# A decoder block on one core: sums' pieces at other steps, each chunk's combination tied to its own place, w_out's raw rows in four buffers

## The chip, the core and the metric

The kernel runs on one core of one Trainium2 chip. The metric is the device time of one execution in microseconds (us), from start to end; less is better. A core has five engines, each with its own instruction queue that is worked strictly in order: TensorE (PE, matrix products), VectorE (DVE), ScalarE (ACT), GpSimd (POOL) and SyncE (SP, which here only issues transfers). Transfers (DMAs) can be issued from the queues of SP, ACT and POOL. Engines wait for each other only through semaphores; a waiting instruction holds up everything behind it in its queue.

## What is computed

The reference is a decoder block with model width 1024 and 2048 tokens, all in float32:

```python
h = _rmsnorm(x, norm_pre_mix)
proj = h @ w_in                                  # q, k, v, u, z, gate_a, gate_b
y_attn = dilated attention of q, k, v            # 3 patterns x 4 heads, merged by softmax of the log-denominators
y_gmlp = gelu(u) * (causal 128x128 mix of layernorm(gelu(z)))
merged = sigmoid(gate_a) * (y_attn @ w_branch_attn) + sigmoid(gate_b) * (y_gmlp @ w_branch_gmlp)
x = x + _rmsnorm(merged @ w_out, norm_post_mix)
h = _rmsnorm(x, norm_pre_mlp)
x = x + _rmsnorm(relu(h @ w_mlp_in) ** 2 @ w_mlp_out, norm_post_mlp)
```

The three attention patterns each leave their own output, maximum and denominator per token. They are combined at the end: `y_attn = sum over patterns of softmax(log-denominator) * output`.

## The kernel before, in words

**Products.** A float32 operand is cut into a high and a low half (`split`, L67: a rounded copy on ACT or POOL, then a subtraction on DVE or POOL at L78), and a product is three matmuls (high x high, high x low, low x high; L95 to L97). The gates' and the MLP's products save one in eight with sums of operand blocks, which have to be made first.

**Order.** PE's instructions run in the order in which the Python code issues them (L56). The other engines' queues are ordered by a planner, which takes what is ready first in its own model of time; `with behind():` (L174) narrows this: every instruction in the block is queued after the last one that the code had issued on the same engine.

**Stages around the change.**

1. Projections. `v_block` (L338) computes v for 128 tokens, `qk_pair` (L301) one third of q or k for 512 tokens. Tokens come in four chunks c = 0 to 3 of 512, and the two halves (chunks 0 and 1, then 2 and 3) are done one after the other.
2. Beside them the **sums** for the gates are made in pieces. `pre_s` (L447) takes a part of w_in (one load of 512 KB on SP, four DVE additions at L455 to L458, two stores on POOL's queue), `pre_t` (L431) the same for the normalized input (two loads of 256 KB, four DVE additions at L439 to L442, one store). Each is a generator of three parts: load, add, store. `pre_step` (L469), inside `behind()`, starts the next piece's load, does the additions of the piece before and the store of the one before that. The list `makers` (L465) has 28 pieces, and eight more (for the first half's input) are put behind it at L519. `while flow: pre_step()` (L517) does all that is left of the 28 when the projections are through.
3. The **filler** (`filler`, L739): u (64 steps), z of the second half (two chunks of 32 steps, `z_chunk`, L565), the gates (505 steps) and z of the first half (64 steps). A step is three matmuls of 128x512. `spatial` (L522) loads the gMLP's mixing weights `wsp`, masks them on POOL (L533) and, after 72 steps of filler, lets PE make a row sum of them (L538). `sz_out` (L547) mixes a normalized chunk of z; it is issued late in the next chunk.
4. **Attention** (`attn_unit`, L830): 48 units, between whose parts steps of the filler are put, so that PE has something to do while the softmax runs. What is left of the gates then, 75 steps, stands beside the **combination** (`combine`, L933), one generator for each chunk: first part, three loads of 528 KB (L937); second part, the weights and the weighted sum (about twenty DVE instructions and an exp on ACT, L940 to L957, then two additions of 128x1024 at L959 and L960, on DVE for chunks 1 and 2, on POOL for 0 and 3); third part, eight PE transposes (L965), a copy on ACT (L967) and a store.
5. **The gates' own work.** `gates` (L661) goes through 126 blocks t of four steps. Block t loads the raw weights of block t + 4 (`piece`, L608), splits those of block t + 3 (`split_piece`, L625), and after its matmuls adds its result on DVE (L723 to L729) or copies it on ACT; results are stored at the end of the next block (L711). From `LAST` = 116 on, each block takes a PSUM bank of its own, of four.
6. **Merge** (`merge`, L1106): for each of eight column tiles dt of a chunk, 18 matmuls, gating on DVE (L1120, L1122). In the first chunk's merge w_out is fetched and split too (`spatial_out`, L1405, which calls `split_wo`, L1063): raw rows of 128x1024 into two buffers "y1", the next load when a buffer is free. From L1139 on `out_block` multiplies by w_out.

Of the kernel before, what the change touches and what calls it, by code (L numbers as in the profile page):

```python
# [16 lines left out]
P = 128  # L17
S = 2048
D = 1024
# [22 lines left out]
def block_kernel(ctx, tc, a, out):  # L42
# [319 lines left out]
    with ExitStack() as e1a:  # L362
# [102 lines left out]
        makers = [lambda n=n, k=k: pre_s(n, k) for n in range(10) for k in (0, 2)]  # L465
        makers[12:12] = [lambda z=z: pre_t(*z) for z in halves[1]]
        flow = []
# [13 lines left out]
        for half in range(2):  # L481
# [4 lines left out]
            for n, (c, i) in enumerate(mine):  # L486
                nb = mine[n + 1] if n + 1 < len(mine) else None
                between = None
                if nb and not (half and nb[0] == 2):
                    if nb != (0, 1):  # L490
                        prenorm_rows(*nb)
                    between = lambda nb=nb: prenorm_cols(*nb)
                v_block(rp, wv, c, i, between)
                if (c, i) == (0, 1):
                    first.close()
# [3 lines left out]
            for n, (g, which) in enumerate(qk):  # L499
# [14 lines left out]
                pre_step()  # L514
                if half and n % 3 == 2:
                    pre_step()
        while flow:  # L517
# [107 lines left out]
    def split_piece(t):  # L625

        if t >= len(seq):
            return
        if t == 4:
            g_["spots"].append(wp.tile([P, 4, 2, 4, P], F32R, name="spots1", tag="w", bufs=3))  # L630
        at_ = t % 4 if t >= LAST else t % 8
        w = g_["spots"][at_ // 4][:, at_ % 4]
        split(w[:, 0], w[:, 1], g_["raw"].pop(t).rearrange("p (k c) -> p k c", k=4),
              "act" if t < 12 or t > LAST - 10 else "pool", "pool")
        g_["w"][t] = w
# [25 lines left out]
    def gates():  # L661
# [75 lines left out]
        yield  # L737

    def filler():  # L739

        for q, (wi, kind, n, half) in enumerate(queue):
# [11 lines left out]
            if kind == "z":  # L753
                if not half:
                    reload_h(1)
                for ci in range(2):
                    for k, _ in enumerate(z_chunk(zps[half], w, half * 2 + ci)):
                        yield
                        if half and k == 10 and (makers or flow):
                            pre_step()  # L760
                    if half and not ci:
                        gates_ahead()
                continue
            for c in (2, 3):
                for m in range(2):
                    p = psum_mm(f"u_{n}{m}{c}")
                    yield from steps_T(w, m, c, p)
                    t = st.tile([P, 512], F32, name=f"ut_{n}{m}{c}", tag="ev", bufs=3)
                    act.activation(t, p, AF.Gelu_apprx_tanh)
                    sp.dma_start(u_d[n * 2 + m, :, c * 512:(c + 1) * 512], t)  # L770
                    pre_step()

# [160 lines left out]
    def combine(c):  # L933
# [20 lines left out]
        for i in range(4):  # L954
            for g in range(3):
                o = A[:, i, g, 0:256].rearrange("p (j e) -> p j e", j=4)
                dve.tensor_tensor(o, o, widen(E[:, i, g, :], 64), op=OP.mult)  # L957
        eng = dve if c in (1, 2) else pool
        eng.tensor_add(A[:, :, 0, :256], A[:, :, 0, :256], A[:, :, 1, :256])  # L959
        eng.tensor_add(A[:, :, 0, :256], A[:, :, 0, :256], A[:, :, 2, :256])  # L960
        yield
# [57 lines left out]
    cs = [combine(c) for c in (2, 3, 0, 1)]  # L1019
    for n in range(2):  # L1020
        for z in cs:
            next(z)
    for n in range(4):
        steps((40, 12, 12, 11)[n])
        next(cs[n])
    ec.close()
# [32 lines left out]
    def load_wo(k):  # L1059
        wo_raw[k] = bot.tile([P, D], F32, name=f"woraw{k}", tag="y1", bufs=2)  # L1060
        (sp if k < 2 else pool).dma_start(wo_raw[k], a["w_out"][:, k, :])

    def split_wo(k):  # L1063
        split(wo[k][:, 0], wo[k][:, 1], wo_raw.pop(k))
        if k + 2 < KT:
            load_wo(k + 2)

# [337 lines left out]
    def spatial_out(dt):  # L1405
# [4 lines left out]
        if dt == 1:  # L1410
            ez.close()
            mgp.append(stack(e2, "mg1", 1))
            ttp = stack(e2r, "ttp", 2, side="right")
        split_wo(dt)
        if dt == KT - 1:
# [591 lines left out]
```

## Time and profile before

| what | value |
|---|---|
| three runs | 2676.23, 2681.05 and 2683.57 us, median 2681.05 |
| the profiled execution: its own time | 2676.26 us |
| its span, first to last instruction | 2674.5 us (1.8 us lie around it) |
| PE busy | 2621.4 us, 12458 matmuls |
| DVE, ACT, POOL busy | 1677.4, 1077.5 and 1196.8 us |
| moved by DMA | 521.99 MB, mean 195 GB/s |
| mean granted TensorE clock | 0.993 |

Times in the trace are us from the first instruction. A row of the timeline has the start, the duration, the engine, the line of the kernel, the operation and `out<-in` by the program's names, then the number of instructions that were merged into the row, and in square brackets how long the engine had been idle before it and what ended that. SPq is SP's queue of transfers; its durations are those of issuing. A row of waits has: who waited, for whom, us in total, times, the longest. A row of windows has the stretch and its length, then busy us and (number) for PE, PEld (weight loads), DVE, ACT and POOL, then the granted clock, the DMA share and GB/s.

### The profile page before, as it was taken

To read this page: it belongs to the slowest core of one execution; us is meant where nothing else is said; L and a number is where in the kernel's file an instruction comes from. 1 tells how busy PE (TensorE), PEld (TensorE's weight loads), DVE (VectorE), ACT (ScalarE), POOL (GpSimd) and SP (SyncE) were. 2 spreads that over 40 slices of the span, in tenths; PEclk is the share of its full clock that TensorE was granted. 3 is DMA by queue.
4 is the path that set the end of the run, shared out by engine and by line. 5 is a ranking of instruction groups with operands and counts; after the bars stand their busy time and mean duration, and the time that the engine had idled before them with its cause. 6 is when DMAs were issued, how large, how long until landed. Compare 5 with 4: busy or idle time off the path is not lost. (4 is left out here: it accounts for less than half of the span.)

```text
span 2674.5 us, 35483 instructions
## 1 busy us (share of the span) xinstructions
PE 2621.4 (98%) x12458; PEld 2188.0 (82%) x12458; DVE 1677.4 (63%) x2881; ACT 1077.5 (40%) x2184; POOL 1196.8 (45%) x1078
## 2 busy tenths in 40 slices
PE   9999999899999978999999999999999999999998
PEld 8888888788888867788878788888888888888886
DVE  5675565445544556665676665655437888888866
ACT  5213111244455332354445555555545333233334
POOL 0362354365455544310333464223315776676645
PEclk9999999999999999999999999999999999999999
DMA  8778668888898987743666464654343212222235
GB/s 322 279 248 276 246 227 280 271 277 261 293 287 237 240 260 271 267 165 136 213 224 255 130 224 153 209 155 129 106 147 117 87 57 86 87 87 87 87 111 212
DMA packets 387843, 521.99 MB, mean 195 GB/s; under 512 B 56849, under 2 KB 241937, under 8 KB 385874
## 3 DMA queue, kind: packets, MB, share of 16 engines
q1 hardware_dynamic: 300048, 431.84, 49.2%
q0 software_dynamic: 14992, 51.65, 5.0%
q10 hardware_dynamic: 72626, 36.25, 4.5%
q8 instruction: 98, 1.61, 0.2%
q14 instruction: 79, 0.65, 0.1%
HBM read 340.67 MB, written 178.98 MB: 194 GB/s over the span
## 5 line engine op out<-in xcount | busy, mean ns | idle before, releaser
L1858 PE MATMUL ya<-T_spots,s 128*128 128x512 f32 x1176 | 289.3, 389 | 0.7 <-ACT T_spots L70 0.5
L70 ACT ACTIVATE s<-sraw 128x768 fp32r<-128x768 f32 (+1 forms) x184 | 127.2, 696 | 330.4 <-POOL sraw L1659 156.1
L1858 PEld LDWEIGHTS ya<-T_spots,s 128*128 128x128 f32 x1176 | 220.5, 188 | 47.4 <-ACT T_spots L70 0.9
L78 DVE TENSOR_TENSOR s<-sraw,s 128x512 fp32r<-128x512 f32 x172 | 184.5, 1097 | 8.5 <-ACT s L70 7.2
L698 PE MATMUL g<-opA,spots 128*128 128x512 f32 x672 | 171.8, 400 | 12.7 <-DVE ga L723 12.7
L1333 PE MATMUL aa<-B,A 128*128 128x512 f32 x768 | 182.4, 390 | 0.9 <-DVE A L85 0.7
L1304 POOL TENSOR_TENSOR s<-w1r 128x512 f32<-128x512 f32 x32 | 42.3, 1322 | 309.8 <-DVE S L78 263.1
L698 PE MATMUL g<-opB,spots 128*128 128x512 f32 x648 | 168.3, 403 | 6.1 <-DVE gx L729 4.6
L1333 PEld LDWEIGHTS aa<-B,A 128*128 128x128 f32 x768 | 143.9, 188 | 31.4 <-DVE A L85 1.1
L1858 PE MATMUL yc<-T_spots,s 128*128 128x512 f32 x624 | 159.6, 389 | 0.0
L698 PEld LDWEIGHTS g<-opA,spots 128*128 128x128 f32 x672 | 122.2, 190 | 35.1 <-issue 13.1
L95 PE MATMUL x<-hT_a,wq 128*128 128x512 f32 x384 | 149.7, 390 | 0.0
L96 PE MATMUL x<-hT_a,wq 128*128 128x512 f32 x384 | 149.4, 389 | 0.0
L97 PE MATMUL x<-hT_a,wq 128*128 128x512 f32 x384 | 149.4, 389 | 0.0
L78 POOL TENSOR_TENSOR spots<-gr,spots 128x512 fp32r<-128x512 f32 x98 | 130.3, 1335 | 41.3 <-ACT spots L70 26.7
L698 PEld LDWEIGHTS g<-opB,spots 128*128 128x128 f32 x648 | 118.6, 192 | 29.5 <-issue 5.0
L1858 PEld LDWEIGHTS yc<-T_spots,s 128*128 128x128 f32 x624 | 117.1, 188 | 24.3
L70 ACT ACTIVATE hl<-r 128x512 fp32r<-128x512 f32 x48 | 30.4, 633 | 240.2 <-POOL r L322 89.0
L1658 POOL TENSOR_TENSOR sraw<-sraw 128x256 f32<-128x256 f32 x56 | 41.9, 748 | 161.5 <-DVE s L78 158.5
L72 POOL TENSOR_SCALAR wq<-wq_r 128x1024 fp32r<-128x1024 f32 x24 | 31.5, 1317 | 184.1 <-PE va L97 133.4
L929 DVE TENSOR_REDUCE o<-po 128x256 f32<-128x512 f32 x48 | 33.2, 692 | 121.2 <-PE po L928 121.2
L78 POOL TENSOR_TENSOR T_spots<-w2r,T_spots 128x512 fp32r<-128x512 f32 x70 | 104.5, 1522 | 7.3 <-ACT T_spots L70 7.3
(412 smaller groups left out, 6988.8 us busy)
## 6 DMA issues: line engine op xcount, KB each, us to landing
w1r<-in_w_mlp_in_dram SPq DMA_DIRECT2D x64, 512.0 KB, 3.7
sraw<-sd SPq DMA_DIRECT2D x128, 256.0 KB, 3.3
qk<-hl SPq DMA_DIRECT2D x24, 1024.0 KB, 5.5
qq<-qk SPq DMA_DIRECT2D x96, 256.0 KB, 5.0
w2r<-in_w_mlp_out_dram SPq DMA_DIRECT2D x16, 1024.0 KB, 7.7
sd<-u ACTq DMA_DIRECT2D x63, 256.0 KB, 2.9
g<-gated SPq DMA_DIRECT2D x58, 256.0 KB, 3.7
gr<-sgd SPq DMA_DIRECT2D x53, 256.0 KB, 4.7
```

Of the source, the lines that this page charges most:

```text
L70: act.activation(hi, src, AF.Copy)
L72: pool.tensor_scalar(hi, src, 1.0, 1.0, op0=OP.mult, op1=OP.mult)
L78: (pool if lo_eng == "pool" else dve).tensor_sub(lo, src, f32(hi))
L95: pe.matmul(ps, lh, rh, start=start, stop=False)
L96: pe.matmul(ps, lh, rl, start=False, stop=False)
L97: pe.matmul(ps, ll, rh, start=False, stop=stop)
L698: pe.matmul(p, w[:, l, k], h[:, r, k], start=i in (1, 6, 5, 4) and not k and not m, stop=k == 3 and m == 2, skip_group_check=True)
L929: dve.tensor_reduce(ot[:, :, j * 64:(j + 1) * 64], po.rearrange("p (b h e) -> p b e h", b=4, h=2), axis=AX.X, op=OP.add)
L1304: pool.tensor_add(s1, a21, a22)
L1333: pe.matmul(p, w[:, l, k, :], h[:, r, k, :], start=i in (1, 6, 5) and not k and not n, stop=k == 3 and n == 2, skip_group_check=True)
L1658: pool.tensor_add(a22, a21, a22)
L1858: pe.matmul(p, s[:, l], w[r], start=i in (1, 2, 5) and not m and not o, stop=m == 1 and o == 2, skip_group_check=True)
```

## The change

It has three parts.

- **Sums.** The pieces of the second half's input stand at places 16 to 23 of `makers`, not 12 to 19. `pre_step` is also called after every second `v_block` of the second half (4 calls more) and no longer twice extra in the second half's q and k (2 calls fewer). In the filler a helper `paced` calls it after every 12th step of u and z, where it was called after every 8th step of u and once in each of the two chunks of z; both make ten calls.
- **Combination.** All four chunks' loads are still issued at the end of attention. The second parts, which all four came right behind, now come at 28, 38, 48 and 58 of the 75 steps, the third parts at 42, 52, 63 and 75 (before: 40, 52, 64, 75), each inside `behind()`. The additions are cut in two: four of 128x512 in place of two of 128x1024. Three rounded copies (blocks 107 to 109) go from ACT to POOL.
- **w_out.** Raw rows 2 and 3 (and 6 and 7) get two buffers "tt" of the pool `ttp`, which is opened at dt = 1 in the place of z's buffers; rows 4 and 5 are loaded when rows 0 and 1 are split.

```diff
@@ -463,7 +463,7 @@
 
         halves = [[(h_, k, j) for k in range(4) for j in range(2)] for h_ in range(2)]
         makers = [lambda n=n, k=k: pre_s(n, k) for n in range(10) for k in (0, 2)]
-        makers[12:12] = [lambda z=z: pre_t(*z) for z in halves[1]]
+        makers[16:16] = [lambda z=z: pre_t(*z) for z in halves[1]]
         flow = []
 
         def pre_step():
@@ -491,6 +491,8 @@
                         prenorm_rows(*nb)
                     between = lambda nb=nb: prenorm_cols(*nb)
                 v_block(rp, wv, c, i, between)
+                if half and i % 2:
+                    pre_step()
                 if (c, i) == (0, 1):
                     first.close()
             nxt = load_w(0, f"wq00{half}")
@@ -512,8 +514,6 @@
                     between = lambda i: prenorm_cols(2, i)
                 qk_pair(rp, w, g, which, 2 * half + 1, ropes[2 * half + 1], between)
                 pre_step()
-                if half and n % 3 == 2:
-                    pre_step()
         while flow:
             pre_step()
         makers += [lambda z=z: pre_t(*z) for z in halves[0]]
@@ -631,7 +631,7 @@
         at_ = t % 4 if t >= LAST else t % 8
         w = g_["spots"][at_ // 4][:, at_ % 4]
         split(w[:, 0], w[:, 1], g_["raw"].pop(t).rearrange("p (k c) -> p k c", k=4),
-              "act" if t < 12 or t > LAST - 10 else "pool", "pool")
+              "act" if t < 12 or t > LAST - 7 else "pool", "pool")
         g_["w"][t] = w
 
     def operand(half, i, slot):
@@ -736,6 +736,16 @@
         sp.dma_start(*out_.pop())
         yield
 
+    paces = [0]
+
+    def paced(gen):
+
+        for _ in gen:
+            yield
+            paces[0] += 1
+            if paces[0] % 12 == 0 and (makers or flow):
+                pre_step()
+
     def filler():
 
         for q, (wi, kind, n, half) in enumerate(queue):
@@ -754,21 +764,17 @@
                 if not half:
                     reload_h(1)
                 for ci in range(2):
-                    for k, _ in enumerate(z_chunk(zps[half], w, half * 2 + ci)):
-                        yield
-                        if half and k == 10 and (makers or flow):
-                            pre_step()
+                    yield from paced(z_chunk(zps[half], w, half * 2 + ci))
                     if half and not ci:
                         gates_ahead()
                 continue
             for c in (2, 3):
                 for m in range(2):
                     p = psum_mm(f"u_{n}{m}{c}")
-                    yield from steps_T(w, m, c, p)
+                    yield from paced(steps_T(w, m, c, p))
                     t = st.tile([P, 512], F32, name=f"ut_{n}{m}{c}", tag="ev", bufs=3)
                     act.activation(t, p, AF.Gelu_apprx_tanh)
                     sp.dma_start(u_d[n * 2 + m, :, c * 512:(c + 1) * 512], t)
-                    pre_step()
 
     fill = filler()
 
@@ -955,9 +961,10 @@
             for g in range(3):
                 o = A[:, i, g, 0:256].rearrange("p (j e) -> p j e", j=4)
                 dve.tensor_tensor(o, o, widen(E[:, i, g, :], 64), op=OP.mult)
-        eng = dve if c in (1, 2) else pool
-        eng.tensor_add(A[:, :, 0, :256], A[:, :, 0, :256], A[:, :, 1, :256])
-        eng.tensor_add(A[:, :, 0, :256], A[:, :, 0, :256], A[:, :, 2, :256])
+        for i in range(0, 4, 2):
+            for g in range(1, 3):
+                eng = dve if c in (1, 2) else pool
+                eng.tensor_add(A[:, i:i + 2, 0, :256], A[:, i:i + 2, 0, :256], A[:, i:i + 2, g, :256])
         yield
         for m in range(2):
             pt = psum_aux(f"yt_{c}{m}")
@@ -1017,12 +1024,12 @@
     ec = ExitStack()
     cb = stack(ec, "cb", 2, side="right")
     cs = [combine(c) for c in (2, 3, 0, 1)]
-    for n in range(2):
-        for z in cs:
-            next(z)
-    for n in range(4):
-        steps((40, 12, 12, 11)[n])
-        next(cs[n])
+    for z in cs:
+        next(z)
+    for n, k in ((28, 0), (10, 1), (4, 0), (6, 2), (4, 1), (6, 3), (5, 2), (12, 3)):
+        steps(n)
+        with behind():
+            next(cs[k])
     ec.close()
     ega.close()
 
@@ -1057,13 +1064,14 @@
     wo_raw = {}
 
     def load_wo(k):
-        wo_raw[k] = bot.tile([P, D], F32, name=f"woraw{k}", tag="y1", bufs=2)
+        wo_raw[k] = ttp.tile([P, D], F32, name=f"woraw{k}", tag="tt") if k % 4 > 1 else \
+            bot.tile([P, D], F32, name=f"woraw{k}", tag="y1", bufs=2)
         (sp if k < 2 else pool).dma_start(wo_raw[k], a["w_out"][:, k, :])
 
     def split_wo(k):
         split(wo[k][:, 0], wo[k][:, 1], wo_raw.pop(k))
-        if k + 2 < KT:
-            load_wo(k + 2)
+        if k + 4 < KT:
+            load_wo(k + 4)
 
     def load_y(c, engs=("act", "dve")):
         cs = slice(c * 512, (c + 1) * 512)
@@ -1411,6 +1419,8 @@
             ez.close()
             mgp.append(stack(e2, "mg1", 1))
             ttp = stack(e2r, "ttp", 2, side="right")
+            load_wo(2)
+            load_wo(3)
         split_wo(dt)
         if dt == KT - 1:
             gpost = bot.tile([P, D], F32, name="gpost")
```

## The prediction

> **What bounds the kernel now.** I read the page first, then PE's waits, then windows of 10 us around each wait, then the queues there.
>
> ```profile
> PE 2621.4 (98%) x12458; PEld 2188.0 (82%) x12458; DVE 1677.4 (63%) x2881; ACT 1077.5 (40%) x2184; POOL 1196.8 (45%) x1078
> ```
> ```profile
> PE g L698 <- DVE ga L723: 12.7, 1, 12.7
> PE rowsum L538 <- POOL wsp L533: 5.2, 1, 5.2
> PE g L698 <- DVE gx L729: 4.6, 1, 4.6
> PE b L95 <- DVE g L1120: 4.0, 2, 2.2
> ...
> PE sz L552 <- DVE z L580: 2.4, 1, 2.4
> ```
> ```profile
> 470.00:480.00 10.00, 4.82 (x13) 2.92 (x12) 0.17 (x1) 2.26 (x4) 1.02 (x4) 0.73 0.90 303
> 480.00:490.00 10.00, 10.00 (x42) 8.20 (x41) 4.84 (x12) 1.61 (x3) 4.91 (x6) 0.92 0.98 344
> ...
> 510.00:520.00 10.00, 7.65 (x39) 6.68 (x38) 9.46 (x27) 3.16 (x5) 1.62 (x3) 0.83 0.83 293
> ...
> 1000.00:1010.00 10.00, 6.15 (x20) 5.01 (x21) 10.00 (x22) 1.27 (x2) 5.34 (x3) 0.64 0.47 131
> ...
> 1800.00:1850.00 50.00, 50.00 (x222) 41.40 (x222) 28.84 (x38) 27.61 (x47) 17.17 (x12) 1.00 0.46 134
> ```
>
> PE is the bound: it idles for 2674.5 - 2621.4 = 53 us, so no rearrangement can win much more than 2%. The change removes no matmul. It can only win or lose waits, and it touches the places of these five: the row sum and sz (sums), the gates' two (combination), and half of b (w_out).
>
> A wait costs more than its idle time. The clock in the windows' third-last column falls behind each of these. At half speed a window's mean is 1 minus half its slow share, so 0.73 means 5.4 us slow up to 480; PE, which went on at 476.9 (the row sum's row below), worked 3.1 us of it and, by 0.92, another 1.6 us. Half of 4.7 us is lost: 2.3 us. Likewise 0.83 around the sz wait is 3.4 us slow, 1.7 lost, and 0.64 means slow until 1007.2, behind a wait that ended at 1003.85 (below): 1.7 more. An undisturbed matmul takes 50 / 222 = 0.225 us, a step of filler 0.68.
>
> The Trainium skill ("TensorE: Matmul & The Clock Gate", section "What's actually happening") has the clock fall after an idle window of about 3.4 us. By it the sz wait of 2.4 us would be followed by no slow stretch and the sum below would be 1.7 us smaller; the row of 510 to 520 shows one, and the row decides.
>
> **Sums: what goes.**
>
> ```profile
> 437.34 10.41 SPq L451 DMA_DIRECT2D ps<-in_w_in_dram  x3
> ...
> 464.75 0.42 DVE L455 TENSOR_TENSOR ps<-ps 128x256 f32<-128x256 f32 x1 [7.29 <-DMA ps<-in_w_in_dram]
> ...
> 468.02 0.69 SPq L528 DMA_DIRECT2D wsp<-in_w_spatial_dram  x1
> ...
> 475.81 1.02 POOL L533 TENSOR_SCALAR_AFFINE_SELECT wsp<-wsp 128x128 f32<-128x128 f32 x4 [7.10 <-DMA wsp<-in_w_spatial_dram]
> ...
> 476.89 2.07 PE L538 MATMUL rowsum<-wsp,ones 128*128 128x512 f32 x2 [5.18 <-POOL wsp L533]
> ...
> 475.58 3.87 SPq L436 DMA_DIRECT2D pt<-hTd  x6
> ...
> 507.46 0.42 DVE L439 TENSOR_TENSOR pt<-pt 128x256 f32<-128x256 f32 x1 [6.12 <-DMA pt<-hTd]
> ```
>
> Before, the projections make 12 + 12 + 2 = 26 calls, so the loop at L517 starts the last two pieces in one burst: SP issues three loads in 10.4 us, DVE waits 7.3 us for the last, and wsp's load, next in SP's queue behind the gates' weights that wait for DVE, goes out only at 468.0 and is masked at 475.8. PE wants it at 471.7 (476.9 less 5.2). Also the pieces of the first half's input start no earlier than 475.6, three at a time, though their first call stands 64 steps before the row sum, at 471.7 - 64 x 0.68 = 428: they are called every 5.4 us, and the buffers that they take over come free only when the burst is stored. DVE then waits 6.1 us at 507 for a piece, with chunk 2's layer norm queued behind it, and PE for that.
>
> After: 12 + 4 + 12 = 28 calls, one per piece, so the loop only drains two pieces: 8 additions and 4 stores, no load. wsp's load moves ahead by at least the 7.3 us that DVE waited, to 461 or earlier, with 10 us to spare against a landing of 7. The input's pieces can then start some 20 us earlier, and come every 12 x 0.68 = 8.2 us, the additions one call after the load, which is more than the 5.1 us in which such a load lands (below). I take both waits as gone: 5.2 + 2.3 + 2.4 + 1.7 = **11.6 us**. Bounds: nothing gone, 0; and no more than 11.6, since these are all the waits on what this part moves.
>
> ```profile
> 260.00:270.00 10.00, 10.00 (x61) 8.81 (x61) 5.18 (x13) 5.21 (x13) 0.00 (x0) 1.00 0.37 133
> ps<-in_w_in_dram SPq DMA_DIRECT2D x20, 512.0 KB, 6.8
> pt<-hTd SPq DMA_DIRECT2D x32, 256.0 KB, 5.1
> ```
>
> The four added calls in `v_block` each issue a 512 KB load, two stores and 4 x 0.42 us on DVE. There DVE is busy 5.2 of 10 us, POOL not at all, the DMA share is 0.37 and PE never waits: hidden, 0. Were that cover gone, a piece's 6.8 us of landing would stand before v's copies once: 6.8 us.
>
> **Combination: what goes and what comes.**
>
> ```profile
> 973.29 15.21 SPq L937 DMA_DIRECT2D A<-att  x12
> ...
> 979.92 0.18 DVE L940 TENSOR_TENSOR M<-A 128x16 f32<-128x16 f32 x1 [1.61 <-DMA A<-att]
> ...
> 983.98 4.10 DVE L957 TENSOR_TENSOR A<-A,E 128x256 f32<-128x256 f32 x12
> ...
> 988.00 1.21 DVE L959 TENSOR_TENSOR A<-A 128x1024 f32<-128x1024 f32 x1
> ...
> 990.05 0.39 SPq L711 DMA_DIRECT2D gated<-ga  x1
> gated<-ga SPq DMA_DIRECT2D x12, 256.0 KB, 3.5
> ...
> 1000.62 2.46 POOL L959 TENSOR_TENSOR A<-A 128x1024 f32<-128x1024 f32 x1 [6.79 <-DVE A L957]
> ...
> 1000.96 2.15 DVE L940 TENSOR_TENSOR M<-A 128x16 f32<-128x16 f32 x1
> ...
> 1003.03 0.68 DVE L723 TENSOR_TENSOR ga<-ga,g 128x512 f32<-128x512 f32 x1
> ...
> 1003.85 4.53 PE L698 MATMUL g<-opA,spots 128*128 128x512 f32 x12 [12.67 <-DVE ga L723]
> ...
> 1028.17 1.45 DVE L960 TENSOR_TENSOR A<-A 128x1024 f32<-128x1024 f32 x1
> ...
> 1048.29 1.04 PE L965 MATMUL yt<-ident,A 128*128 128x128 f32 x8
> ...
> 1049.08 0.48 PE L95 MATMUL z<-w_z,hT_b 128*128 128x512 f32 x1
> ```
>
> DVE works off four combinations from 979.9 to 1029.6, 49.7 us, nearly without idle, with the gates' additions between. Block 113's addition, ready at 988.5 (991.2, when PE stopped, less one block of 2.7), stands behind them and runs at 1003.0; PE waits 12.7 us. Without waits PE would have needed, from the end of attention at 970.8 (988.5 less 26 steps), 75 x 0.68 and four times 1.04 for transposes: to 1026. It began z at 1049.1: 23 us lost.
>
> After, the second part of chunk 2 is tied behind 28 steps, that is, behind block 113's addition (430 of the gates' 505 steps are done at the end of attention; block 113 ends with step 456, 26 on). That addition still needs its buffer: block 109's store stands behind the twelve loads of A on SP (issued at 990.05, and 3.5 us to land, the median of this stage). So about 994.5 the tied work starts. Its own size: 4 x (2.0 small + 4.1) + 2 x 2.4 on DVE = 29.2 us; the old 49.7 hold this, eight additions (5), one split of z's weights (1.2), 2 us of waiting for exp, and 12 us by which DVE's small operations were stretched beside POOL (M, 0.18 alone, 2.15 beside POOL's 2.46). All of these come again: the halves change 2 x 1.21 into 4 x about 0.69, and POOL has the same elements. PE's last transposes stand behind the last of it: 994.5 + 49.7 = 1044.2, plus 1.0 for them, 1045.2. Against 1049.1 that is **3.9 us** won: the 12.7 shrinks to about 3, and waits at the transposes take its place, which is what is late next.
>
> What a tied DVE instruction holds up: the additions of blocks 114 to 121; for them wait PE (a bank is used again four blocks, 10.8 us, later, about as long as one combination), SP's stores, and behind those SP's loads of blocks 120 to 125. Bounds: DVE's stretch gone, the tied work ends at 1032 and PE is at 1033 (16 us won); or the exps of four chunks held on ACT behind copies that wait for such loads:
>
> ```profile
> 1032.27 0.63 ACT L70 ACTIVATE spots<-ga 128x512 fp32r<-128x512 f32 x1 [6.04 <-DMA ga<-sgd]
> ...
> 1040.83 0.63 ACT L70 ACTIVATE spots<-ga 128x512 fp32r<-128x512 f32 x1 [7.93 <-DMA ga<-sgd]
> ```
>
> At 7 us each this makes 28, an end at 1073, 24 us lost. I take 3.9, nearest to the chain that was measured. Three copies (0.63) go to POOL before the combination, where it waits anyway: 0.
>
> **w_out.**
>
> ```profile
> 1109.09 0.61 POOL L1061 DMA_DIRECT2D woraw<-in_w_out_dram  x1 [1.80 <-DVE gates L1120]
> ...
> 1114.59 0.74 DVE L559 SCALAR_TENSOR_TENSOR sb<-sz,lngb,bsp 128x512 f32<-128x512 f32 x1
> ...
> 1120.44 1.06 ACT L70 ACTIVATE wo<-woraw 128x1024 fp32r<-128x1024 f32 x1 [4.69 <-DMA woraw<-in_w_out_dram]
> ...
> 1125.14 0.69 DVE L562 TENSOR_TENSOR sb<-sb,ur 128x512 f32<-128x512 f32 x1 [2.39 <-DMA ur<-ud]
> ```
>
> ACT's waits for raw rows (4.7 us here) go for rows 4 to 7. But rows 2 and 3 now wait for z's place: bsp there is read until 1115.3, so row 2, fetched at 1109.1 before, comes 6 us later, and 512 KB more are under way when DVE waits for ur, which is what PE's 2.2 us hang on. Gain at most 2.2, loss at most those 6 us less the 2 that the banks hold, 4. I take 0, both in one queue.
>
> **Sum.** 11.6 + 3.9 + 0 = 15.5; 2676.3 - 15.5 = 2660.8 for an execution like the profiled one, which lies 4.8 below the median of the runs: **2665.6**.
>
> **Rivals.**
>
> 1. *The combination hides fully.* For it: the additions that PE waited for now stand ahead of the tied work. Against: DVE had no idle time to give. 11.6 + 16 = 27.6: 2653.5.
> 2. *The sums' waits stay.* The pieces are as many; in 437 to 471 the 28-call version starts four pieces of the first half's input where two of w_in are gone, so wsp may land as late. Against: DVE's 7.3 us are gone from the path. 3.9 alone: 2677.2. Beside it the Trainium skill ("Trainium Kernel Development and Optimization", "Key Constraints") says that all queues' transfers share the same 16 DMA engines; by that, spacing frees nothing unless bytes leave the stretch.
> 3. *The ties starve each other (slower).* Each chunk's exp stands on ACT behind a copy for block t + 3, that behind a load, that behind a store that waits for a tied addition. For it: the two ACT rows above. Against: those loads need additions from four blocks earlier. Break-even at (3.9 + 11.6) / 4 = 3.9 us per chunk; at 7 us, 2665.6 + 28 = 2693.6.
>
> **Numbers.** Forecast 0.5 (its own range 2659 to 2673), rival 1 0.22, rival 2 0.18, rival 3 0.10. A measurement of this kernel can tell about 0.3% (8 us) from no change. Faster: 0.5 + 0.22 + a fifth of rival 2 = 0.76; same: the rest of it and rival 3's milder end, 0.17; slower 0.07. The range takes in most of rivals 1 and 2 and w_out's bounds: 2649 to 2683.
>
> **What would show it.** Right: no row "rowsum <- wsp" and no "sz <- z" among PE's waits; pt's loads from about 455 on, and by 480 one at a time; the wait at ga L723 near 3 us; waits at yt L965, z starting near 1034 (1045 less the sums' 11.6). Wrong: wsp issued after 465; DVE idle between tied combinations with exp as releaser (rival 3), or M at 0.18 throughout (rival 1); a longer wait at b L95.

## The result, and the profile after the change

The changed kernel takes **2672.2 us** (median of 14 runs, 2669.0 to 2679.8) against 2681.1 us before (14 runs): 8.9 us less, a ratio of 0.9968 with a 95% interval from 0.9959 to 0.9977. Its profiled execution took 2673.3 us with a span of 2671.6, that is 3.0 us less than the profiled execution before (that one lay 4.8 below its kernel's median, this one lies 1.1 above). Where the text below compares rows of two profiles, it uses the place of one and the same matmul in both.

The page and PE's waits of the changed kernel (in us: total, times, longest):

```profile
PE 2619.7 (98%) x12458; PEld 2187.3 (82%) x12458; DVE 1679.4 (63%) x2885; ACT 1076.3 (40%) x2181; POOL 1201.8 (45%) x1085
```
```profile
PE yt L972 <- POOL A L967: 8.4, 2, 6.5
PE g L698 <- DVE M L946: 6.6, 1, 6.6
PE po L934 <- ACT pvs L930: 4.7, 1, 4.7
PE yt L972 <- issue: 4.1, 1, 4.1
```

The rows for the row sum (5.2 us) and sz (2.4 us) are gone. The gates' 12.7 us are 6.6 now, put down to DVE's M: that instruction follows the addition for which PE waits, so it is the same place. The gates' second wait of before (gx, 4.6 us) is gone too. New are the waits at yt, the combination's transposes, of 8.4 and 4.1 us, and one of 2.9 us for the gates' weights. At the row sum and at sz the granted clock (the third-last column, 1.00 here) no longer falls either; windows of the kernel after the change:

```profile
470.00:480.00 10.00, 10.00 (x44) 7.91 (x43) 3.42 (x9) 3.62 (x6) 5.85 (x6) 1.00 0.98 330
...
510.00:520.00 10.00, 10.00 (x46) 8.26 (x45) 5.76 (x8) 4.97 (x8) 5.54 (x6) 1.00 0.50 174
```

The timeline there (start, duration, instruction, in brackets the idle time before it and its releaser):

```profile
441.25 0.69 SPq L528 DMA_DIRECT2D wsp<-in_w_spatial_dram  x1
...
450.37 1.02 POOL L533 TENSOR_SCALAR_AFFINE_SELECT wsp<-wsp 128x128 f32<-128x128 f32 x4 [5.63 <-DMA wsp<-in_w_spatial_dram]
451.23 2.49 SPq L436 DMA_DIRECT2D pt<-hTd  x4
...
472.21 1.02 PE L538 MATMUL rowsum<-wsp,ones 128*128 128x512 f32 x2
...
474.23 8.45 SPq L436 DMA_DIRECT2D pt<-hTd  x6
...
492.88 1.92 DVE L580 TENSOR_SCALAR z<-z,mv,r_ln 128x512 f32<-128x512 f32 x4
...
501.95 0.42 DVE L439 TENSOR_TENSOR pt<-pt 128x256 f32<-128x256 f32 x1 [5.34 <-DMA pt<-hTd]
...
505.75 3.73 PE L552 MATMUL sz<-wsp,z 128*128 128x128 f32 x32
```

wsp is masked at 450, 22 us before PE wants it. The last piece's wait on DVE is nearly as long as it was (5.3 us against 6.1), but the layer norm that sz needs is done at 494.8 and no longer stands behind it.

PE's place against the kernel before, in the two profiles: 11.4 us ahead behind sz, 8.6 behind attention's last transposes (a wait for pvs, which the change doesn't touch, was 4.7 us against 3.25 and was followed by slow clock), 3.8 at the start of z, 3.0 at the end. So the sums won 11.4 us, and the **combination lost 4.8**. Its timeline after the change:

```profile
961.91 20.70 PE L698 MATMUL g<-opA,spots 128*128 128x512 f32 x90
964.72 15.19 SPq L943 DMA_DIRECT2D A<-att  x12
...
981.47 0.39 SPq L711 DMA_DIRECT2D gated<-ga  x1
...
988.39 0.69 DVE L723 TENSOR_TENSOR ga<-ga,g 128x512 f32<-128x512 f32 x1 [5.06 <-DMA gated<-ga]
989.00 0.17 DVE L946 TENSOR_TENSOR M<-A 128x16 f32<-128x16 f32 x1
...
1009.79 7.31 POOL L967 TENSOR_TENSOR A<-A 128x512 f32<-128x512 f32 x4 [2.50 <-DVE A L963]
...
1010.84 0.50 SPq L622 DMA_DIRECT2D ga<-sgd  x1
...
1027.21 0.33 SPq L91 DMA_DIRECT2D w_z_r<-in_w_in_dram  x1
...
1041.55 2.48 DVE L967 TENSOR_TENSOR A<-A 128x512 f32<-128x512 f32 x4
1043.54 2.09 PE L972 MATMUL yt<-ident,A 128*128 128x128 f32 x8 [4.07 <-issue]
1045.28 0.78 PE L95 MATMUL z<-w_z,hT_b 128*128 128x512 f32 x1
```

Block 113's addition (L723 at 988.4) waits for block 109's store, which SP issues only behind the twelve loads of A. The tied chain runs from 989.0 to 1044.0, 55 us, and the last transposes stand right behind its last half.

### The profile page after: what moved, and what is told of

Read it like the earlier page. It is cut to its first block, busy times and chain, and to the rows that moved or that the text cites. A ratio compares the mean times of both kernels' runs of the same rounds, so it can differ in the third digit from the quotient of the medians.

```text
span 2671.6 us, 35481 instructions
## 1 busy us (share of the span) xinstructions
PE 2619.7 (98%) x12458; PEld 2187.3 (82%) x12458; DVE 1679.4 (63%) x2885; ACT 1076.3 (40%) x2181; POOL 1201.8 (45%) x1085
## 5 line engine op out<-in xcount | busy, mean ns | idle before, releaser
L72 POOL TENSOR_SCALAR spots<-gr 128x512 fp32r<-128x512 f32 x78 | 48.5, 622 | 127.5 <-PE g L698 94.8
```

Of the source, the lines that this page charges most:

```text
L72: pool.tensor_scalar(hi, src, 1.0, 1.0, op0=OP.mult, op1=OP.mult)
```

## The experiments

Their measure, beside the time, is **the stretch**: from PE's first gate matmul behind attention's last transposes (961.91 above) to z's first matmul (1045.28), 83.4 us after the change. It leaves out what was won or lost before attention's end. Before the change it began with this row of the timeline, and with z at 1049.08 it was 78.6 us:

```profile
970.48 3.70 PE L698 MATMUL g<-opA,spots 128*128 128x512 f32 x15
```

Idle is the sum of PE's gaps in the stretch, and the next columns say when DVE's part of the combination begins and ends, counted from the start of the stretch.

A stretch is read from one profiled execution of each kernel. The four kernels that keep the combination of before (before, e1, e3 and e4) show how far it scatters: 78.0 to 81.6 us. A difference of less than 3.6 us between two rows of the table is therefore not shown to come from an edit.

| kernel | ratio to before (95%) | stretch, us | PE idle | DVE's part |
|---|---|---|---|---|
| before | 1 | 78.6 | 18.8 | 9.4 to 59.1 |
| after | 0.9968 (0.9959 to 0.9977) | 83.4 | 21.9 | 27.1 to 82.1 |
| e1 sums | 0.9949 (0.9932 to 0.9966) | 78.7 | 19.2 | 9.5 to 59.2 |
| e2 combination | 1.0010 (0.9998 to 1.0022) | 83.8 | 22.5 | 27.1 to 82.5 |
| e3 w_out | 1.0002 (0.9988 to 1.0016) | 78.0 | 18.2 | 10.1 to 59.6 |
| e4 sums, w_out | 0.9961 (0.9945 to 0.9976) | 81.6 | 20.2 | 9.8 to 59.2 |
| e5 loads of A spread | 0.9963 (0.9949 to 0.9977) | 84.7 | 20.9 | 22.6 to 81.9 |
| e6 whole additions | 0.9960 (0.9947 to 0.9974) | 83.5 | 23.1 | 27.2 to 82.5 |
| e7 no ties | 0.9951 (0.9937 to 0.9965) | 79.3 | 17.7 | 9.4 to 63.6 |
| e8 all on DVE | 0.9952 (0.9940 to 0.9965) | 81.5 | 20.5 | 27.1 to 80.8 |
| e9 spread, DVE | 0.9960 (0.9945 to 0.9975) | 81.3 | 18.2 | 23.3 to 77.7 |
| e10 no ties, spread | 0.9980 (0.9969 to 0.9991) | 83.5 | 21.7 | 9.6 to 61.7 |
| e12 no ties, spread, DVE | 0.9965 (0.9951 to 0.9979) | 81.5 | 19.0 | 9.7 to 60.8 |
| e13 no elementwise work | 0.9903 (0.9887 to 0.9920) | 69.1 | 9.9 | none |

The theory to begin with: the sums gave what was forecast, and the combination lost because its chain starts late, behind block 113's addition. Rivals: POOL's additions in halves, or the ties themselves.

**The parts alone.** e1 takes the hunks of the sums only:

```diff
-        makers[12:12] = [lambda z=z: pre_t(*z) for z in halves[1]]
+        makers[16:16] = [lambda z=z: pre_t(*z) for z in halves[1]]
...
+                if half and i % 2:
+                    pre_step()
...
-                if half and n % 3 == 2:
-                    pre_step()
...
+    paces = [0]
+    def paced(gen):
...
```

> Only the first part of the change: the pieces of the sums spaced out; combination and w_out as before. The prediction's step for this part says 11.6 us: by it the time is 11 to 12 us below the kernel before (ratio 0.9957), with no row 'rowsum <- wsp' and no 'sz <- z' among PE's waits, and the 12.7 us wait on block 113's addition still there. Theory (the sums gave what was forecast and the combination gave part of it back): 10 to 12 us below the kernel before, so 1 to 3 us faster than the whole change. Rival (the parts only add up differently: what is won early is given back by later waits that are tied to the stream of DMAs, whatever the combination does): 8 to 9 us below, as the whole change.

Measured: 2670.7 us, 12.0 below the kernel before by the medians of these runs, 13.7 by the ratio (9 to 18). In the trace PE is 11.4 us ahead behind sz, as after the whole change, and keeps it through the combination (11.9 us at z). The long wait of the gates is as it was before; the wait at b will be needed below (PE's waits, e1):

```profile
PE g L698 <- DVE ga L723: 12.8, 1, 12.8
...
PE b L95 <- DVE g L1126: 2.3, 4, 1.2
```

This is the theory's 10 to 12 us; the rival's 8 to 9 lie just outside the interval. e2 takes the combination's hunks only:

```diff
-              "act" if t < 12 or t > LAST - 10 else "pool", "pool")
+              "act" if t < 12 or t > LAST - 7 else "pool", "pool")
...
-        eng = dve if c in (1, 2) else pool
-        eng.tensor_add(A[:, :, 0, :256], A[:, :, 0, :256], A[:, :, 1, :256])
-        eng.tensor_add(A[:, :, 0, :256], A[:, :, 0, :256], A[:, :, 2, :256])
+        for i in range(0, 4, 2):
+            for g in range(1, 3):
...
+    for n, k in ((28, 0), (10, 1), (4, 0), (6, 2), (4, 1), (6, 3), (5, 2), (12, 3)):
+        steps(n)
+        with behind():
+            next(cs[k])
```

> Only the second part: the combination tied and in halves, and the copies of three pieces on POOL. The prediction's step says 3.9 us won. Theory (the tied chain starts behind block 113's addition, whose buffer comes free only behind the twelve loads of A, and PE's transposes wait for each chunk): 2 to 7 us lost at the start of z against the kernel before, and a time of 0 to 6 us above it, a part of it caught up in the later waits. Rival (the loss in the whole change comes from what the sums' spacing does to the combination): 2 to 5 us below the kernel before.

Measured: 2685.3 us, 1.0010 of before, an interval that holds no change and excludes the 3.9 us (0.9985) that the prediction's step would have won. The stretch is 83.8 us, 5.2 longer than before; the waits are those of the whole change (PE's waits, e2):

```profile
PE yt L966 <- POOL A L961: 9.3, 2, 7.4
PE g L698 <- DVE M L940: 6.7, 1, 6.7
...
PE b L95 <- DVE g L1121: 2.8, 3, 1.3
```

So the longer stretch comes with the second part alone and doesn't need the sums' spacing; the time shows only that this part doesn't win. e3 takes the hunks of w_out only:

```diff
-        wo_raw[k] = bot.tile([P, D], F32, name=f"woraw{k}", tag="y1", bufs=2)
+        wo_raw[k] = ttp.tile([P, D], F32, name=f"woraw{k}", tag="tt") if k % 4 > 1 else \
+            bot.tile([P, D], F32, name=f"woraw{k}", tag="y1", bufs=2)
...
-        if k + 2 < KT:
-            load_wo(k + 2)
+        if k + 4 < KT:
+            load_wo(k + 4)
```

> Only the third part: the raw rows of w_out in four places. The prediction's step says 0, bounds 2.2 us won and 4 us lost. Theory: within 2 us of the kernel before, with the waits of ACT for raw rows 4 to 7 gone and PE's waits at b L95 about as long. Rival: the rows' 512 KB more under way delay the loads that the merge waits for, 2 to 4 us above it.

Measured: 2681.9 us, 1.0002. The longest wait at b fell from 2.2 to 1.4 us, and one at o of 1.9 us is new (PE's waits, e3):

```profile
PE b L95 <- DVE g L1121: 2.5, 3, 1.4
PE o L95 <- DVE g L1121: 1.9, 1, 1.9
```

The fall at b is not shown to be this part's: e1 and e2, which leave w_out alone, have it too, with 1.2 and 1.3 us for the longest (their rows above). The wait at o is: 1.9 to 2.8 us in every profile with the four buffers, and no such row in the three without them (before, e1, e2).

e4 has both the sums' and w_out's hunks, and the combination of before.

> The whole change without its second part. Theory: 9 to 12 us below the kernel before, that is 0 to 3 us faster than the whole change, since the combination loses about 6.5 us at the start of z and gets back most of them in the waits that follow. By the prediction's step for the combination this kernel would be 3.9 us slower than the whole change, 5 us below the kernel before.

Measured: 2670.8 us, 0.9961 of before, 1.4 us less than the whole change by the medians. That fits the theory and contradicts the prediction's step (5 us below before); the intervals of e4 and of the whole change overlap, so the times alone don't show the loss. The stretches speak for it: 78.0 to 81.6 in four kernels without the second part, 83.4 and 83.8 in the two with it, though e4 lies only 1.8 us from the whole change.

**What in the combination costs.** Four kernels change one thing each of the whole change. Their expectations name z's place in the execution, but attention ended at 957 to 964 us in these four and at 961.9 after the change, so the text goes by the stretch. By z's place alone (1041.7, 1040.3, 1043.5 and 1040.8 against 1045.3) all four look better. e5 issues the loads of A in three groups:

```diff
-    for z in cs:
-        next(z)
-    for n, k in ((28, 0), (10, 1), (4, 0), (6, 2), (4, 1), (6, 3), (5, 2), (12, 3)):
+    next(cs[0])
+    next(cs[1])
+    for n, ks in ((14, (2,)), (14, (3, 0)), (10, (1,)), (4, (0,)), (6, (2,)), (4, (1,)), (6, (3,)), (5, (2,)),
+                  (12, (3,))):
         steps(n)
         with behind():
-            next(cs[k])
+            for k in ks:
+                next(cs[k])
```

> The whole change, but the loads of A are not issued in one block of twelve: six (chunks 2 and 3) where all twelve stood, three 14 steps later, three 28 steps later. Theory (the tied chain starts 9 us late because block 109's store, which frees the place that block 113's addition writes, stands on SP behind twelve loads that take 15.2 us to issue): that store goes out some 7 us earlier, block 113's addition runs near 981 instead of 988.4, PE's wait of 6.6 us there is gone, and z starts 4 to 7 us earlier than 1045.3; time 3 to 7 us below the whole change. Rival (POOL's halves or the ties set the end): z within 2 us of 1045, the waits at the transposes grow by what the first wait loses.

Measured: 2674.0 us, 0.9963, and a stretch of 84.7 us. The wait at block 113 fell from 6.6 to 2.1 us and the chain began 4.5 us earlier in the stretch, as the theory said, but it ended only 0.2 earlier, being 59.3 us long in place of 55.0: the wait at yt grew and one for the gates' weights came in (PE's waits, e5):

```profile
PE yt L972 <- POOL A L967: 10.7, 2, 7.3
PE g L698 <- POOL spots L78: 5.3, 2, 4.7
...
PE g L698 <- DVE M L946: 2.1, 1, 2.1
```

So an earlier start alone didn't help. e6 puts the whole additions back:

```diff
-        for i in range(0, 4, 2):
-            for g in range(1, 3):
-                eng = dve if c in (1, 2) else pool
-                eng.tensor_add(A[:, i:i + 2, 0, :256], A[:, i:i + 2, 0, :256], A[:, i:i + 2, g, :256])
+        eng = dve if c in (1, 2) else pool
+        for g in range(1, 3):
+            eng.tensor_add(A[:, :, 0, :256], A[:, :, 0, :256], A[:, :, g, :256])
```

> The whole change, but each combination's additions run over the whole tile, two of 128x1024, instead of four halves. Theory (late start of the chain): z within 2 us of 1045.3, time within 2 us of the whole change. Rival (the halves are what costs: four took 7.3 us on POOL for chunk 3, and two whole ones 4.9 before): PE's 6.5 us wait for A at the second transposes 2.4 us shorter, POOL's work on chunk 0 shorter by about as much, z 2 to 5 us earlier.

Measured: 2670.7 us, 0.9960, a stretch of 83.5. Two whole additions took 4.9 us on POOL where four halves took 7.3, yet PE stood longer at the second transposes, not shorter (8.8 us against 6.5 and 1.9), and the stretch is the same. So the halves are not shown to cost anything either. e7 keeps places and halves but takes the ties away:

```diff
         steps(n)
-        with behind():
-            next(cs[k])
+        next(cs[k])
```

> The whole change, but the combination's steps are not tied: the same places and halves, each instruction free to be ordered as before. Theory (late start of the chain): without the ties the first chunk's work goes ahead of block 113's addition again, which is late for PE as it was before: a wait of 10 us or more at that addition, and shorter ones at the transposes, z within 3 us of 1045.3 either way. Rival (the ties themselves cost, as one chunk's work can't fill another's waits): z 4 us or more earlier, time 4 us or more below the whole change.

Measured: 2669.5 us, 0.9951; the stretch is 79.4 us, 4.0 shorter than tied. PE waits 11.0 us at block 113's addition again, and not at all at yt (PE's waits, e7):

```profile
PE g L698 <- DVE ga L723: 11.0, 1, 11.0
```

z starts only 1.8 us earlier, since this execution lost more at po (5.4 us against 4.7), and the time is 2.7 us below the whole change's: by the expectation's words the theory is met. By the stretch, which leaves po out, the rival has it. The three copies that the change moves to POOL were not run alone; e7 has them, and its stretch is 0.7 us above that of the kernel before. e8 runs every half on DVE:

```diff
-                eng = dve if c in (1, 2) else pool
+                eng = dve
```

> The whole change, but all halves of the additions run on DVE, those of chunks 3 and 0 too, which were POOL's. DVE gets eight more of about 0.6 us, 5 us. Theory (late start; a chain on DVE that is full from 989 on): the chain is 5 us longer on DVE, the waits for POOL (6.5, 1.9 and 2.9 us on PE) shrink by about as much, z within 3 us of 1045.3. Rival (POOL beside DVE is what stretches the chain: 7.3 us for four halves against 2.5 on DVE, and DVE's small operations 0.7 to 1.4 us instead of 0.2 beside it): z 4 to 9 us earlier, and M and E on DVE near 0.2 throughout.

Measured: 2668.3 us, 0.9952, a stretch of 81.5: 1.9 shorter, between the two and within the scatter. The waits for POOL are gone and others of nearly the same sum, 13.5 us against 12.5, stand at the same transposes (PE's waits, e8):

```profile
PE yt L972 <- issue: 13.5, 3, 7.2
```

By now the first theory had fallen. The next one: the ties keep DVE from the combination for 27 us instead of 9.4, and that is what z pays for; take both the ties and the block of loads away, and the stretch should shrink. e9 is e5 and e8 together (no further edit).

> The whole change, still tied, with the loads of A in three groups and all halves on DVE. So far the stretch from the last transposes of attention (po) to the start of z is 78.0 to 81.6 us in the four kernels whose combination isn't tied by the change, 83.4 to 84.7 in four tied ones, 81.5 with all halves on DVE, 79.4 with the change's places but no ties. Theory, now (the ties keep DVE idle until block 113's addition, 27 us behind po instead of 9.5, and z waits for the end of the chain): the chain starts at 22 to 23 us and is 50 to 53 us long, so the stretch is 74 to 78 us, 4 to 7 less than with the halves on DVE alone. Rival (POOL or the order of SP decides, and the tie is harmless once these are out of the way): below 74 us. Third case (each tied chunk costs its own wait whatever starts it): 80 us or more.

Measured: 2669.6 us, 0.9960, a stretch of 81.3 with DVE's part over at 77.7: the third case. e10 is e7 and e5 together:

```diff
+    next(cs[0])
+    next(cs[1])
+    for n, ks in ((14, (2,)), (14, (3, 0)), (10, (1,)), (4, (0,)), (6, (2,)), (4, (1,)), (6, (3,)), (5, (2,)),
+                  (12, (3,))):
+        steps(n)
+        for k in ks:
+            next(cs[k])
```

> The change's places without ties, with the loads of A in three groups. Theory (untied, DVE starts 9.5 us behind po and has done the combination some 60 us behind it, long before z; what is left is the wait of 11 us for block 113's addition, which hangs on block 109's store behind the loads of A): that wait falls to 4 us or less, the stretch from po to z from 79.4 to 70 to 75 us, time 4 to 9 us below the untied kernel. Rival (DVE is full there in any order, and what that wait loses comes back at the next blocks' additions): 77 to 80 us, time within 2 us of it.

Measured: 2675.1 us, 0.9980, a stretch of 83.5. Neither case: the wait at block 113 halved (11.0 to 5.3), and the stretch grew by 4.1 against e7. In PE's waits, and in SP's and ACT's timeline, it can be seen where it went:

```profile
PE g L698 <- ACT spots L70: 12.1, 2, 8.7
PE g L698 <- DVE ga L723: 5.3, 1, 5.3
```
```profile
1009.07 0.81 SPq L711 DMA_DIRECT2D gated<-gx  x1
1024.48 1.47 SPq L91 DMA_DIRECT2D w_z_r<-in_w_in_dram  x2
1026.00 0.43 SPq L622 DMA_DIRECT2D ga<-sgd  x1
...
1033.12 0.63 ACT L70 ACTIVATE spots<-ga 128x512 fp32r<-128x512 f32 x1 [16.76 <-DMA ga<-sgd]
```

SP stands for 14.6 us at a load of z's weights whose place is not free, and the load of the next gate weights stands behind it in the same queue; PE waits 8.7 us for those. SP's own waits put 12.9 us of this down to DVE, which has yet to split the rows of z's weights that lie in that place.

This is not special to e10. After the change SP stands 15.9 us at the same kind of load (its rows at 1010.84 and 1027.21 are above), and 16.0 us in e2. In e7 it is 7.6 us, and 5.2 in the kernel before, whose rows are:

```profile
1030.25 0.32 SPq L711 DMA_DIRECT2D gated<-gx  x1
1035.74 0.33 SPq L91 DMA_DIRECT2D w_z_r<-in_w_in_dram  x1
```

So this wait may be a part of what the tied order loses; no run tests it alone, and it is not all of it, since in e5 SP stands 8.3 us there and the stretch is the longest of all. e12 adds to e10 that all halves run on DVE.

> As the run before (untied, loads of A in three groups), with all halves on DVE. Theory: 1 to 3 us below the same kernel with POOL's halves, as DVE's multiplications are no longer stretched beside POOL (27 us in the untied kernel, 20 where POOL was still). Rival (DVE is full, 5 us more work on it make each wait for it longer): 2 to 5 us above it.

Measured: 2671.1 us, 0.9965, 4.0 us below e10 by the medians, somewhat more than the theory's 1 to 3; the stretch is 1.9 shorter. Moving POOL's halves to DVE won 1.9, 1.9 and 3.4 us of the stretch in the three pairs (after and e8, e10 and e12, e5 and e9). Each is within the scatter; that all three point one way makes it likely, not shown. For the ties the pairs don't agree: without them the stretch is 4.0 us shorter (after and e7), 1.2 shorter (e5 and e10) and 0.2 longer (e9 and e12).

**Without the work.** In thirteen profiles with the same work, in nine orders, PE was idle for 17.7 to 23.1 us of the stretch. e13 leaves the work itself out: nothing between A's loads and its transposes.

```diff
-        M = sm.tile([P, 4, 4], F32, name=f"M_{c}", tag="cM")
...
-        for i in range(0, 4, 2):
-            for g in range(1, 3):
-                eng = dve if c in (1, 2) else pool
-                eng.tensor_add(A[:, i:i + 2, 0, :256], A[:, i:i + 2, 0, :256], A[:, i:i + 2, g, :256])
         yield
```

> The whole change with the combination's work on DVE, ACT's exp and POOL's additions left out: each chunk of A is loaded, and its first branch is transposed and stored unweighted; loads, places, filler steps and SP's order up to there are the same. Nine arrangements of this work all left PE 17.7 to 23.1 us idle between po and z. Theory A (these elementwise operations are what PE waits for, in whatever order): idle time there falls under 8 us, the stretch from 83.4 to 64 us or less, time 20 us or more below the whole change. Theory B (SP's one queue and the places of its loads set the pace, the loads of A, of the gates' pieces and of z's weights and input standing one behind the other; the elementwise work only chooses where PE waits): 12 us idle or more, the stretch 72 us or more, time at most 11 us below the whole change.

Measured: 2658.2 us, 0.9903, 14.0 us below the whole change by the medians and 17 by the ratios; the stretch is 69.1 us (1038.06 less 969.01), 14.3 shorter, and 9.9 us of it idle. (The profiled execution took 2668.6 us, 10.4 more than the median; it lost 6.8 us at po, ahead of the stretch.) That is between the two theories (PE's waits and timeline, e13):

```profile
PE g L698 <- DVE ga L723: 6.6, 1, 6.6
...
PE g L698 <- ACT spots L70: 2.1, 1, 2.1
...
PE g L698 <- POOL spots L78: 1.2, 1, 1.2
```
```profile
969.01 3.25 PE L698 MATMUL g<-opA,spots 128*128 128x512 f32 x13
...
1038.06 0.48 PE L95 MATMUL z<-w_z,hT_b 128*128 128x512 f32 x1
```

The elementwise work is worth 14.3 us of the stretch in the tied order. By the prediction's count PE would need 75 x 0.68 + 4 x 1.04 = 55.2 us. The other 13.9 us are there without the work: 6.6 us at block 113's addition, with block 109's store behind the loads of A as before, 3.3 us for gate weights that come late, and 4 us by which PE's work is longer, with slow clock behind both waits.

## Why the prediction was right, and where its steps failed

It forecast 15.5 us less and got 8.9, inside its range. The term that carried it was right, the second was wrong in sign, and the third was right at 0 without the gain that was one of its two sides.

- *PE bounds the kernel, its idle time is all there is to win.* Held: PE's busy time is 2619.7 us after and 2621.4 before.
- *Sums, 11.6 us.* Right. 11.4 us by the trace, after the change and in e1, and e1's ratio gives 9 to 18. wsp's load goes out at 441, not just before 461; pt's loads start at 451 (about 455 was said). That the pieces would then come one at a time was wrong: six are issued in a row at 474.2, and DVE still waits 5.3 us for one. The sz wait went for another reason than the spacing near it: the layer norm was done before that piece, at 494.8, 11 us ahead of sz.
- *A wait costs its idle time and slow clock behind it.* Held: without the waits the clock around 475 and 515 is 1.00 in the rows above. It doesn't hold behind every wait (last section).
- *Combination, 3.9 us won.* **Wrong**: 4.8 us lost in the stretch (5.2 in e2). The step took the tied work's start, added the chain's old 49.7 us and found z earlier. In the new profile, 8.6 us ahead at that place, the start should have been 985.9 and was 989.0, since block 109's store took 6.9 us from issue to the addition instead of 3.5; the chain was 55.0 us long instead of 49.7, and the two make 8.4 of the 8.7 us by which z missed its forecast. But mending these sizes doesn't mend the step: in e5 the chain started 4.5 us earlier in the stretch and was 4.3 us longer, and z came no earlier. The step failed where it treated the chain as one length to be shifted. Why the tied order is slower stays open: the pairs with and without ties give 4.0, 1.2 and -0.2 us, and POOL's halves and SP's stand at z's weights are likely parts. What the rows suggest is this: untied, DVE ends its part some 60 us into the stretch and the gates' matmuls fill the rest; tied, the transposes stop PE chunk by chunk, and all that waits in PE's order behind them (additions, stores, loads of weights) comes later too.
- *The ties starve each other (rival 3).* Its mechanism was half right: what came late was the loads behind SP's queue, but its price, 7 us for each chunk, was too high, and the exps were not what PE waited for.
- *Rival 2, the sums' waits stay.* Refuted by the missing rows; *rival 1, the combination hides*, by the stretch.
- *w_out, 0.* Right in the number: e3 is at 1.0002. The loss is there, about 2 us at o. The gain is not shown: b's wait is as short in e1 and e2, without the new buffers. ACT's waits for raw rows fell from 12.0 us to 6.5; they were to go for rows 4 to 7.
- The chance for "faster by over 0.3%" is decided by little: the ratio's interval, 0.9959 to 0.9977, has its middle just beyond that bound.

All versions but e2, e3 and e10 have a ratio below that of the change; the lowest with all the work are e1, e7 and e8, at 0.9949 to 0.9952. All three are faster than the kernel before; against the changed kernel their intervals still touch its own, so that they beat it is likely and not shown. **Open** stays what would shorten the stretch: no order of the same work did. z's weights loaded behind the gates' last pieces, which the rows of SP suggest, weren't tried.

## What to carry to other kernels

Work that is late on one engine should be priced by taking it out before it is moved about: e13 says that 14 us hang on it and 14 us don't, and nine orders of it moved the stretch between 78 and 85. A tie that puts urgent work first also holds back the idle engine time ahead of it, so ask what the engine did there before (here the combination began 17.6 us later in the stretch). And where several streams share one in-order DMA queue, follow the queue: in e10 the 5.7 us that PE no longer waited at block 113 came back at loads that stood behind a place not yet free.

## What the runs showed of the hardware

**A 128x4 instruction can take 2.3 us.** The wait at po, in attention, was between none and 6.8 us in these kernels, though none changes it. In the timeline of the kernel after the change DVE's nm meets a subtraction on POOL and ends with it:

```profile
932.54 2.34 POOL L78 TENSOR_TENSOR opB<-opB 128x1024 fp32r<-128x1024 f32 x1
932.61 2.29 DVE L886 TENSOR_SCALAR nm<-o 128x4 f32<-128x4 f32 x1
```

In e5 the same instruction starts 0.09 us before POOL's and takes 0.16:

```profile
931.47 0.16 DVE L886 TENSOR_SCALAR nm<-o 128x4 f32<-128x4 f32 x1
...
931.56 2.36 POOL L78 TENSOR_TENSOR opB<-opB 128x1024 fp32r<-128x1024 f32 x1
```

Of nm's 48 instructions after the change the median took 0.17 us; twelve took more than 0.5.

The Trainium skill ("SBUF — State Buffer", section "Who interferes with whom") has DVE and GpSimd share one pair of ports: a DVE `tensor_scalar` can run in a mode that uses this pair too, and then whichever engine issued first holds it for the whole instruction and blocks the other. Whether nm runs in that mode no row says, but these rows agree: 0.16 us when DVE was first, POOL's whole remaining time when POOL was.

The exps behind nm, and so PE at po, wait for it: 4.7 us after the change, 2.0 in e5. It is not the only cause. In e3 nm took 0.16 us and PE waited 5.3 us at po, since the addition in front of nm on DVE stood 6.9 us for the store of a block of the gates; after the change it stood 4.7 (first row after the change, second e3):

```profile
932.00 0.69 DVE L723 TENSOR_TENSOR ga<-gx,g 128x512 f32<-128x512 f32 x1 [4.69 <-DMA gated<-ga]
```
```profile
945.69 0.69 DVE L723 TENSOR_TENSOR ga<-gx,g 128x512 f32<-128x512 f32 x1 [6.93 <-DMA gated<-ga]
```

**The clock falls in steps of 3.4 us, also behind short waits.** By the trace's records of the granted clock the slow stretches between 470 and 1140 us were 3.4, 6.8, 10.2, 13.7 or 17.1 us long in all profiles. The Trainium skill ("TensorE: Matmul & The Clock Gate", section "What's actually happening") names a free-running window of about 3.4 us; the steps agree with it, but a wait need not be that long. Behind e5's wait of 2.1 us at 979.9 the window from 980 to 990 shows 0.83, 3.4 us at half speed. Before the change PE waited 3.25 us at po, up to 947.3, and the window behind that shows 1.00 (first row e5, second the kernel before):

```profile
980.00:990.00 10.00, 9.95 (x36) 7.68 (x36) 6.53 (x26) 5.76 (x7) 1.29 (x1) 0.83 0.96 331
```
```profile
947.00:957.00 10.00, 9.74 (x58) 8.47 (x59) 6.04 (x18) 4.92 (x14) 4.80 (x4) 1.00 0.93 325
```

Between 470 and 1140 us of all profiles, waits of 2.0 to 3.3 us had slow clock with them or not, and every wait of more than 3.4 us had it. So the price of a wait of 2 to 3.3 us has two values, and a sum should carry both.
